# Sums of squared keys in four column groups, and two heads in turn in the products that complete T

## The chip, the cores and the metric

The kernel runs on one core of a Trainium2 chip. The core has a matrix engine (TensorE, PE in the profile; its weight loads are PEld), a vector engine (VectorE, DVE), a scalar engine (ScalarE, ACT), GpSimd (POOL), and SyncE (SP), which issues most transfers. The metric is the device time of one execution in microseconds, lower is better; where several runs are given, their median counts.

## What is computed

The reference is a trunk of two residual layers over 512 tokens of width 2048: one of gated differential attention, then one of RWKV-7 time mixing. Only the second layer is touched. It has 32 heads of 64 channels. Cut to what matters here:

```python
kk = heads(k * k_k)
kk = kk / jnp.maximum(jnp.sqrt(jnp.sum(kk * kk, axis=-1, keepdims=True)), 1e-12)
...
def step(S, inp):                       # per head, token after token
    sa = jnp.einsum('bhvk,bhk->bhv', S, a_t)          # a_t = -kk, b_t = kk * a
    S = S * w_t[:, :, None, :] + sa[..., None] * b_t[:, :, None, :] + v_t[..., None] * k_t[:, :, None, :]
    y = jnp.einsum('bhvk,bhk->bhv', S, r_t)
```

## The kernel before

The second layer goes through sixteen *pairs* of heads (`for j in range(D // P)` in `layer1`); a pair fills the 128 partitions, its first head on 0 to 63 and its second on 64 to 127. The 512 tokens are cut into `NC_` = 8 chunks of `C` = 64. For each pair there are:

- four projections of 128 channels (`unit_chan`, products in `mm3`, line 122), each 48 matmuls of 512 columns: fp32 numbers are split into a high and a low part of type fp32r (`split_w`, L105 on ACT and L106 on DVE for weights), and three products are added;
- `stage1`, whose steps `decays`, `exponentials`, `queries`, `scales` and `keys` are put in a list `g.later` and issued one by one behind steps of the scan of the pair before; `keys` squares k (L1264) and splits the square (`split_act`, L1101 on ACT and L1102 on DVE);
- `gram`: it sums the squared keys over the channels of each head with a matrix of ones (`sum_channels`, L1210 and L1211), copies the sums to the tile `ssl` (L1291 on ACT), writes them to a DRAM buffer `ltd` with two transfers on SP (L1293), and then forms the products of keys and queries within each chunk (L1304, tiles `gp`), which ACT copies to `G` (L1311) and SP writes to `ltd` (L1316);
- `t_solve`: POOL loads `ltd` into `LT` (L1350), and DVE divides by the sums (L1352, L1353) and inverts two triangular blocks of 32 per chunk in 31 steps (L1361, L1363). The result goes to DRAM (L1365);
- `t_combine`, one pair later: it loads the blocks into `TT`, transposes them (L1388), and forms the block below the diagonal with two runs of 32 x 32 products: L1394 into `px`, ACT copies to `X` (L1397), L1404 into `px`, ACT copies to `TT` (L1407). ACT also copies `AR` into `G` (L1400), over values that L1394 reads;
- `scan_pair`: for each chunk three products in a row, L1475 (`sm`), L1486 (reads `rhs`, which ACT copies in L1478), L1493, with L1488 on ACT and L1497 on DVE (L1500 for the first chunk) between them; then the outputs (L1515, L1519) and their normalisation.

`t_combine` and `scan_pair` are a `Chain`: they are issued in steps, each after a given number of matmuls of the projections, so that they stand among them on TensorE. From the fifth pair on the steps are placed so that L1394 of one pair, then the sums and L1304 of the next pair, then L1404 stand next to each other, ahead of the first L1475 of the scan.

The order of instructions on each engine is fixed when the kernel is built: a planner takes the instructions by priority (`high_priority`: weights 2000, the chain 3000, the solve and `ssl` 4000, all else by program order) when its own estimate of the times says that they can start; `issue_after` puts an instruction behind another one on its engine. Tiles with one tag share a buffer: `k2`, `ssl` and the `th` of `gate` have the tag `thg` with one buffer, and the split of k2 and that of r times k share `xH` and `xL`.

Of the kernel before, what the change touches and what calls it, by code (L numbers as in the profile page):

```python
# [13 lines left out]
F32 = mybir.dt.float32  # L14
# [3 lines left out]
AF = mybir.ActivationFunctionType  # L18
# [5 lines left out]
P = 128  # L24
D = 2048
T = 512
KT = D // P
NT = T // P
# [1068 lines left out]
def split_act(g, src, pool, tag):  # L1097
    nc = g.nc
    hh = pool.tile(list(src.shape), F32R, name="sH" + tag, tag=tag + "H", bufs=1)
    hl = pool.tile(list(src.shape), F32R, name="sL" + tag, tag=tag + "L", bufs=1)  # L1100
    nc.scalar.copy(hh[:], src)  # L1101
    nc.vector.tensor_sub(hl[:], src, hh[:].bitcast(F32))  # L1102
    return hh, hl
# [33 lines left out]
C = 64  # L1137
NC_ = T // C
HALF = 32
# [67 lines left out]
def sum_channels(g, out, ones, x):  # L1207

    h, l = x
    g.nc.tensor.matmul(out, ones, h[:], start=True, stop=False)  # L1210
    g.nc.tensor.matmul(out, ones, l[:], start=False, stop=True)  # L1211


def stage1(g, j, k, up):


    nc, w = g.nc, g.work
    p = Pair()
    col = lambda n: g.prm[n][:, j : j + 1]
    ch = lambda ap: ap.rearrange("p (c t) -> p c t", c=NC_)  # L1220
    th = []
    for i, nm in enumerate(("hw0", "ha0")):
        (uH, uL), (xH, xL) = up, g.dwda[i]
        ps = g.ps.tile([P, 512], F32, name="pt", tag="pb", bufs=2)
        mm3(nc, ps[:], uH[:, i, :], uL[:, i, :], xH[:], xL[:], True, True)
        o = w.tile([P, T], F32, name=f"th{i}", tag=f"th{i}", bufs=1)
        nc.scalar.activation(o[:], ps[:], AF.Tanh, bias=col(nm), scale=0.5)
        th.append(o)
    lw, tha = th
    nc.scalar.activation(lw[:], lw[:], AF.Identity, bias=g.hdec[:], scale=-0.5 * DECAY)  # L1230
    l = w.tile([P, NC_, C], F32, name="l", tag="l", bufs=1)
    m = g.small.tile([P, NC_], F32, name="m", tag="m", bufs=3)
    p.E = w.tile([P, NC_, C + 1], F32, name="E", tag="E", bufs=1)
    p.gam = g.small.tile([P, NC_], F32, name="gam", tag="gam", bufs=3)
    p.AR = w.tile([P, NC_, 2, C], F32, name="AR", tag="AR", bufs=3)
    p.BK = w.tile([P, NC_, 2, C], F32, name="BK", tag="BK", bufs=1)
    p.f = w.tile([P, T], F32, name="f", tag="f", bufs=1)

    def decays():
        nc.vector.tensor_tensor_scan(l[:].rearrange("p c t -> p (c t)"), g.rmask[:].rearrange("p c t -> p (c t)"),  # L1240
                                     lw[:], 0.0, ALU.mult, ALU.add)
        nc.vector.tensor_scalar(m[:], l[:, :, C - 1], 0.5, None, ALU.mult)
        nc.vector.tensor_sub(l[:], l[:], m[:, :, None].to_broadcast([P, NC_, C]))

    def exponentials():
        nc.scalar.activation(p.E[:, :, 0], m[:], AF.Exp, scale=-1.0)
        nc.scalar.activation(p.E[:, :, 1:], l[:], AF.Exp)
        nc.scalar.activation(l[:], l[:], AF.Exp, scale=-1.0)
        nc.scalar.activation(p.f[:], tha[:], AF.Identity, bias=col("omka"), scale=col("hka"))

    def queries():
        nc.vector.tensor_mul(p.f[:], p.f[:], k[:])
        nc.vector.scalar_tensor_tensor(p.AR[:, :, 0, :], ch(k[:]), col("nkk"), p.E[:, :, 0:C], ALU.mult, ALU.mult)
        nc.vector.tensor_mul(l[:], ch(k[:]), l[:])

    def scales():
        for i in range(2):
            nc.scalar.activation(p.BK[:, :, i, :], ch(tha[:]), AF.Identity, bias=col(f"bk_b{i}"),
                                 scale=col(f"bk_s{i}"))

    def keys():
        nc.vector.tensor_mul(p.BK[:], p.BK[:], l[:, :, None, :].to_broadcast([P, NC_, 2, C]))
        k2 = w.tile([P, T], F32, name="k2", tag="thg", bufs=1)
        nc.scalar.activation(k2[:], k[:], AF.Square, scale=col("kk"))  # L1264
        p.k2 = split_act(g, k2[:], w, "x")
        nc.vector.tensor_add(p.gam[:, 0 : NC_ - 1], m[:, 0 : NC_ - 1], m[:, 1:NC_])
        nc.scalar.activation(p.gam[:, 0 : NC_ - 1], p.gam[:, 0 : NC_ - 1], AF.Exp)

    g.later += [(0, decays), (1, exponentials), (0, queries), (1, scales), (1, keys)]
    return p  # L1270

# [12 lines left out]
def gram(g, j, p, before):  # L1284

    nc, w, BK = g.nc, g.work, p.BK
    ps = g.ps.tile([P, 512], F32, name="pt", tag="pa", bufs=1)
    sum_channels(g, ps[:2, :], g.ones[:, 0 : P : C], p.k2)
    ss = w.tile([2, T], F32, name="ssl", tag="thg", bufs=1)
    with g.tc.high_priority(offset=SOLVE):  # L1290
        nc.scalar.copy(ss[:], ps[:2, :])  # L1291
        for half in range(2):
            nc.sync.dma_start(  # L1293
                out=g.ltd[j % 2, half, :, :, HALF, :],
                in_=ss[:].rearrange("h (c b t) -> h c b t", c=NC_, b=2)[:, :, half, :])
    p.G = w.tile([P, NC_, 2, 2, C], F32, name="G1", tag="G1", bufs=2)
    p.BKT = w.tile([P, NC_, P], F32, name="BKT", tag="BKT", bufs=2)
    halves = []
    for c0, tag in ((0, "pb"), (4, "pc")):
        gp = [g.ps.tile([P, 512], F32, name="gp", tag=tag, bufs=2) for _ in range(2)]  # L1300
        halves.append((c0, gp))
        for i in range(4):
            for h, r_ in ((0, slice(0, C)), (1, slice(C, P))):
                m = nc.tensor.matmul(gp[h][:, i * P : (i + 1) * P], BK[r_, c0 + i, :, :], p.AR[r_, c0 + i, :, :],  # L1304
                                     start=True, stop=True)
    if before:
        with g.tc.issue_after(m.ins):
            before.step(g)
    for c0, gp in halves:
        for h in range(2):  # L1310
            nc.scalar.copy(p.G[:, c0 : c0 + 4, :, h, :], gp[h][:].rearrange("p (u x t) -> p u x t", u=4, x=2))  # L1311
    with g.tc.high_priority(offset=SOLVE if j == D // P - 1 else 0):
        for half in range(2):
            for h in range(2):
                q0 = h * C + half * HALF
                nc.sync.dma_start(  # L1316
                    out=g.ltd[j % 2, half, h, :, 0:HALF].rearrange("c s t -> s c t"),
                    in_=p.G[q0 : q0 + HALF, :, 0, h, half * HALF : (half + 1) * HALF])
# [53 lines left out]
def t_combine(g, j, p, lead):  # L1372

    nc, w, TT = g.nc, g.work, g.TT[j % 2]
    for h in range(2):
        for half in range(2):
            o, l0 = half * HALF, half * 16 + h * NC_
            nc.sync.dma_start(
                out=TT[h * C + o : h * C + o + HALF, :, h, o : o + HALF],
                in_=g.td[j % 2].rearrange("q (g l) t -> (q g) l t", g=NG)[:, l0 : l0 + NC_, :])  # L1380
    T1 = w.tile([P, NC_, HALF], F32, name="T1", tag="T1", bufs=1)
    X = w.tile([P, NC_, HALF], F32, name="X", tag="X", bufs=1)
    px = g.ps.tile([P, 512], F32, name="px", tag="pd", bufs=1)
    yield lead
    for h in range(2):
        r_ = slice(h * C, h * C + C)
        with g.tc.issue_after(g.centred) if g.centred else ExitStack():
            nc.vector.transpose(T1[r_], TT[r_, :, h, 0:HALF])  # L1388
    yield GAP_T
    N = NC_ * HALF  # L1390
    blocks = [(h, h * C, slice(h * C, h * C + HALF), slice(h * C + HALF, h * C + C)) for h in range(2)]
    for h, b0, lo, hi in blocks:
        for c in range(NC_):
            nc.tensor.matmul(px[hi, c * HALF : (c + 1) * HALF], p.G[lo, c, 0, h, HALF:C], T1[lo, c, :],  # L1394
                             start=True, stop=True, tile_position=(b0, b0 + HALF))
    for _, _, _, hi in blocks:
        nc.scalar.copy(X[hi], px[hi, :N].rearrange("p (c s) -> p c s", c=NC_))  # L1397
    for h, b0, _, _ in blocks:
        r_ = slice(b0, b0 + C)
        nc.scalar.copy(p.G[r_, :, 0, h, :], p.AR[r_, :, 0, :])  # L1400
    yield GAP_X
    for h, b0, lo, hi in blocks:
        for c in range(NC_):
            nc.tensor.matmul(px[lo, N + c * HALF : N + (c + 1) * HALF], X[hi, c, :], TT[hi, c, h, HALF:C],  # L1404
                             start=True, stop=True, tile_position=(b0 + HALF, b0))
    for h, b0, lo, _ in blocks:
        nc.scalar.copy(TT[lo, :, h, HALF:C], px[lo, N:].rearrange("p (c s) -> p c s", c=NC_))  # L1407
    yield GAP_T
# [363 lines left out]
```

## Time and profile before

| | |
|---|---|
| runs | 2114.43, 2110.9, 2113.84 us; median 2113.84 |
| profiled execution | 2111.84 us, of which the span from the first to the last instruction is 2110.1 |
| granted TensorE clock | 0.997 of full |
| busy, share of the span | PE 98%, PEld 80%, DVE 76%, ACT 55%, POOL 18% |
| the second layer's pairs | from 955 to 1960 us; a pair takes about 61.5 us from the fifth pair on |

The profile gives each instruction its line, engine, start and duration. In the timeline a row reads: start in us from the start of the span, duration in us, engine, line, operation, tiles written and read, partitions x elements, and the number of instructions that the row merges; in brackets stands the idle time of the engine before it and what ended it. A matmul's duration is its whole way through the array, and the next one starts before it ends, so what a matmul costs is read from one start to the next. A product in fp32 shows as two rows, two halves of the work; one in fp32r as one. "PEld ... LDWEIGHTS" is the load of a matmul's stationary operand.

### The profile page before, as it was taken

The page shows a single profiled execution, that of the slowest core. Times are in us where ns is not written, and L with a number is a line of the kernel's source. Part 1 is how long each engine was busy: PE and PEld are TensorE (multiplying, and loading weights), DVE is VectorE, ACT ScalarE, POOL GpSimd, SP SyncE. Part 2 cuts the span into 40 slices and gives each one's busy share as a digit, 9 for nine tenths or more (in the row PEclk, how much of TensorE's full clock was granted, in tenths as well). Part 3 has the DMA queues.
Part 4 walks back from the last instruction along what each step waited for, and adds up shares of the span by engine and source line. Part 5 has one row for each costly group of instructions (what it writes and reads, how often), then busy time and mean ns, then how long its engine had stood idle before and what let it go on. Part 6 is the DMA issues. An engine that isn't in the chain of part 4 may idle for free.

```text
span 2110.1 us, 34038 instructions
## 1 busy us (share of the span) xinstructions
PE 2076.8 (98%) x11852; PEld 1690.5 (80%) x11852; DVE 1602.6 (76%) x4129; ACT 1153.6 (55%) x2278; POOL 370.4 (18%) x727
## 2 busy tenths in 40 slices
PE   9999999999999999999999999999999999999999
PEld 7888888888887788878777778888877787877887
DVE  6988888889887876576777778877777887767645
ACT  5765656566565544355465555565555556555322
POOL 1021111201112000101122221222222122221001
PEclk9999999999999999999999999999999999999999
DMA  8487877878778946623232332323333232345655
GB/s 268 153 173 190 181 170 187 166 188 177 173 183 176 307 149 179 150 88 96 90 87 89 90 90 84 94 83 92 99 95 86 85 94 86 97 138 180 190 159 121
DMA packets 159484, 294.60 MB, mean 140 GB/s; under 512 B 64352, under 2 KB 81760, under 8 KB 159312
## 3 DMA queue, kind: packets, MB, share of 16 engines
q1 hardware_dynamic: 110848, 184.91, 28.1%
q0 software_dynamic: 23808, 83.54, 21.5%
q10 hardware_dynamic: 24656, 23.97, 3.5%
q8 instruction: 93, 1.52, 0.3%
q14 instruction: 79, 0.65, 0.1%
HBM read 268.71 MB, written 23.66 MB: 139 GB/s over the span
## 4 chain that ended last, share of the span: by engine, by line
PE 74%; DVE 17%; issue 3%; ACT 3%; DMA 2%; ACTq 0%; DVEq 0%; SPq 0%
PE pp L122 33%; PE pp L568 22%; PE pt L122 4%; DVE wl L106 4%; DVE tmpl L1361 3%; DVE Tm L1363 2%; DVE VS L1497 2%; PE gp L1304 1%; ACT wh L105 1%; PE sc L122 1%; PE o L122 1%; PE sm L1475 1%; PE lora L122 1%; PE z L122 1%; PE sm L1486 1%
## 5 line engine op out<-in xcount | busy, mean ns | idle before, releaser
L106 DVE TENSOR_TENSOR wl<-wraw,wh 128x1024 fp32r<-128x1024 f32 (+2 forms) x291 | 357.7, 1229 | 211.0 <-ACT wh L105 202.2
L105 ACT CAST wh<-wraw 128x1024 fp32r<-128x1024 f32 (+2 forms) x291 | 303.6, 1043 | 266.1 <-PE pp L122 135.2
L122 PE MATMUL pp<-hL,wh 128*128 128x512 f32 x1024 | 414.7, 405 | 0.0
L122 PE MATMUL pp<-hH,wh 128*128 128x512 f32 x1024 | 413.8, 404 | 0.0
L122 PE MATMUL pp<-hH,wl 128*128 128x512 f32 x1024 | 413.6, 404 | 0.0
L122 PEld LDWEIGHTS pp<-hH,wh 128*128 128x128 f32 x1024 | 193.6, 189 | 34.3
L122 PEld LDWEIGHTS pp<-hL,wh 128*128 128x128 f32 x1024 | 193.5, 189 | 33.3
L122 PEld LDWEIGHTS pp<-hH,wl 128*128 128x128 f32 x1024 | 193.6, 189 | 32.4
L568 PE MATMUL pp<-wh,hH 128*128 128x512 f32 x448 | 176.8, 395 | 0.0
L568 PE MATMUL pp<-wh,hL 128*128 128x512 f32 x448 | 175.8, 392 | 0.0
L122 PE MATMUL pp<-wh,hH 128*128 128x512 f32 x372 | 145.6, 392 | 1.8 <-ACT hH L1092 1.8
L122 PE MATMUL pp<-wh,hL 128*128 128x512 f32 x372 | 146.4, 394 | 0.2
L122 PE MATMUL pp<-wl,hH 128*128 128x512 f32 x372 | 145.9, 392 | 0.5 <-DVE wl L106 0.5
L1481 POOL COPY SA<-VS 64x64 f32<-64x64 f32 x224 | 69.9, 312 | 425.0 <-DVE VS L1497 386.0
L1361 DVE SCALAR_TENSOR_TENSOR tmpl<-LT,Tm 128x60 f32<-128x60 f32 (+24 forms) x496 | 133.6, 269 | 11.4
L568 PE MATMUL pp<-wl,hH 128*128 128x512 f32 x448 | 140.4, 392 | 0.0
L1363 DVE TENSOR_TENSOR Tm<-Tm,tmpl 128x60 f32<-128x60 f32 (+24 forms) x496 | 104.4, 211 | 11.3
L1478 ACT COPY rhs<-sm 64x64 f32<-64x64 f32 x256 | 52.8, 206 | 89.3 <-PE sm L1475 85.9
L568 PEld LDWEIGHTS pp<-wl,hH 128*128 128x128 f32 x448 | 84.4, 188 | 17.3
L568 PEld LDWEIGHTS pp<-wh,hH 128*128 128x128 f32 x448 | 84.2, 188 | 17.3 <-issue 0.3
L568 PEld LDWEIGHTS pp<-wh,hL 128*128 128x128 f32 x448 | 84.2, 188 | 16.3
L1488 ACT COPY VS<-sm 64x64 f32<-64x64 f32 x256 | 52.7, 206 | 71.9 <-PE sm L1486 67.3
(397 smaller groups left out, 4417.6 us busy)
## 6 DMA issues: line engine op xcount, KB each, us to landing
wraw<-in_rw_w_in_dram SPq DMA_DIRECT2D x128, 512.0 KB
wraw<-in_da_w_in_dram SPq DMA_DIRECT2D x75, 512.0 KB
wraw<-in_da_w_in_dram POOLq DMA_DIRECT2D x28, 512.0 KB, 6.6
wraw<-in_da_w_out_dram SPq DMA_DIRECT2D x26, 512.0 KB
wraw<-in_rw_w_out_dram SPq DMA_DIRECT2D x26, 512.0 KB
Ta<-in_da_w_in_dram POOLq DMA_DIRECT2D x21, 512.0 KB, 5.5
Tb<-in_da_w_in_dram POOLq DMA_DIRECT2D x21, 512.0 KB, 5.5
Tc<-in_da_w_in_dram POOLq DMA_DIRECT2D x21, 512.0 KB, 5.5
```

The source lines that it names most:

```text
L105: a = nc.scalar.copy(hi[:, ks], raw[:, ks])
L106: d = nc.vector.tensor_sub(lo[:, ks], raw[:, ks], hi[:, ks].bitcast(F32))
L122: m = nc.tensor.matmul(out, a, b, start=s, stop=e, skip_group_check=skip)
L568: m = nc.tensor.matmul(out[t][:], x, wt[lo][:, k, :], start=first, stop=end and lo == 1 and k == KG - 1, skip_group_check=True)
L1304: m = nc.tensor.matmul(gp[h][:, i * P : (i + 1) * P], BK[r_, c0 + i, :, :], p.AR[r_, c0 + i, :, :], start=True, stop=True)
L1361: nc.vector.scalar_tensor_tensor(tt, LT[:, i : i + 1, i + 1 :].to_broadcast([P, s, n]), n2[:, i : i + 1], Tm[:, 0:s, i : i + 1].to_broadca ...
L1363: nc.vector.tensor_add(Tm[:, 0:s, i + 1 :], Tm[:, 0:s, i + 1 :], tt)
L1475: nc.tensor.matmul(sm[:, 0:P], both(p.G[:, c, 0]), both(VS[:, c]), start=True, stop=True)
L1478: nc.scalar.copy(rhs[r_, :], sm[r_, h * C : h * C + C])
L1481: nc.gpsimd.tensor_copy(p.SA[r_, c - 1, :], VS[r_, c, h, :])
L1488: g.copied = nc.scalar.copy(VS[r_, c, h, :], sm[r_, P : P + C])
L1497: g.state = nc.vector.scalar_tensor_tensor(VS[r_, c + 1, h, :], s_, p.gam[r_, c : c + 1], Sg[r_, :], ALU.mult, ALU.add)
```

## The change

Two things are changed in the second layer.

The squared keys are no longer split into two fp32r parts. They stay fp32, in a tile of their own (`k2`), and are summed by four fp32 products, one for each 128 tokens, instead of two fp32r products over 512 tokens. Each product has 32 columns of the ones matrix as its stationary operand (16 for each head) and goes to its own group of 32 columns of the array, so that the sums of tokens 128 t to 128 t + 127 land on partitions 32 t to 32 t + 31. The copy `ssl` is then 128 partitions x 128 elements, also in a tile of its own, and the two transfers to `ltd` take one head each, from four partitions, instead of one half of each chunk.

In `t_combine` the loops of the two runs of products are exchanged: chunk after chunk, and in each the first head, then the second, instead of all chunks of the first head before those of the second. The products themselves and their places are the same.

```diff
     def keys():
         nc.vector.tensor_mul(p.BK[:], p.BK[:], l[:, :, None, :].to_broadcast([P, NC_, 2, C]))
-        k2 = w.tile([P, T], F32, name="k2", tag="thg", bufs=1)
-        nc.scalar.activation(k2[:], k[:], AF.Square, scale=col("kk"))
-        p.k2 = split_act(g, k2[:], w, "x")
+        p.k2 = w.tile([P, T], F32, name="k2", tag="k2", bufs=1)
+        nc.scalar.activation(p.k2[:], k[:], AF.Square, scale=col("kk"))
...
     ps = g.ps.tile([P, 512], F32, name="pt", tag="pa", bufs=1)
-    sum_channels(g, ps[:2, :], g.ones[:, 0 : P : C], p.k2)
-    ss = w.tile([2, T], F32, name="ssl", tag="thg", bufs=1)
+    for t in range(NT):
+        nc.tensor.matmul(ps[t * 32 : t * 32 + 32, :P], g.ones[:, C - 16 : C + 16].bitcast(F32),
+                         p.k2[:, t * P : (t + 1) * P], start=True, stop=True, tile_position=(0, t * 32))
+    ss = w.tile([P, P], F32, name="ssl", tag="ssl", bufs=1)
     with g.tc.high_priority(offset=SOLVE):
-        nc.scalar.copy(ss[:], ps[:2, :])
-        for half in range(2):
+        nc.scalar.copy(ss[:], ps[:, :P])
+        for h in range(2):
             nc.sync.dma_start(
-                out=g.ltd[j % 2, half, :, :, HALF, :],
-                in_=ss[:].rearrange("h (c b t) -> h c b t", c=NC_, b=2)[:, :, half, :])
+                out=g.ltd[j % 2, :, h, :, HALF, :].rearrange("b (q c) t -> q c b t", q=NT),
+                in_=ss[16 * h : P : 32, :].rearrange("q (c b t) -> q c b t", c=2, b=2))
...
-    for h, b0, lo, hi in blocks:
-        for c in range(NC_):
+    for c in range(NC_):
+        for h, b0, lo, hi in blocks:
             nc.tensor.matmul(px[hi, c * HALF : (c + 1) * HALF], p.G[lo, c, 0, h, HALF:C], T1[lo, c, :],
                              start=True, stop=True, tile_position=(b0, b0 + HALF))
...
-    for h, b0, lo, hi in blocks:
-        for c in range(NC_):
+    for c in range(NC_):
+        for h, b0, lo, hi in blocks:
             nc.tensor.matmul(px[lo, N + c * HALF : N + (c + 1) * HALF], X[hi, c, :], TT[hi, c, h, HALF:C],
                              start=True, stop=True, tile_position=(b0 + HALF, b0))
```

## The prediction

> **What bounds the kernel now.** I read the page first, then busy time by stretches, then the waits, then the timeline of one period.
>
> ```profile
> PE 2076.8 (98%) x11852; PEld 1690.5 (80%) x11852; DVE 1602.6 (76%) x4129; ACT 1153.6 (55%) x2278; POOL 370.4 (18%) x727
> 1434.00:1495.50 61.50, 60.82 (x422) 49.39 (x420) 46.48 (x133) 35.00 (x78) 15.24 (x35) 1.00 0.30 90
> PE sm L1475 <- DVE VS L1497: 7.6, 22, 0.6
> ```
>
> The second row is one pair of heads of layer two: 61.5 us, PE (first count) busy for 60.8, DVE (third) 46.5, ACT (fourth) 35.0. The third row is the only wait of PE that the waits view lists from 1188 to 1860 us, 7.6 us in eleven periods. So TensorE looks like the bound, and what the change takes from it should come off the time. Before adding that up I looked at the stretch in which the changed lines run:
>
> ```profile
> 1495.43 0.39 PE L122 MATMUL pp<-hH,wl 128*128 128x512 f32 x1
> 1495.75 1.09 PE L1394 MATMUL px<-T,G 32*32 32x32 f32 x32
> 1496.48 0.62 ACT L1400 COPY G<-AR 64x512 f32<-64x512 f32 x1 [3.15 <-PE px L1394]
> 1496.78 0.40 PE L1210 MATMUL pt<-sHx,ones 128*2 128x512 f32 x1
> 1497.01 0.40 PE L1211 MATMUL pt<-sLx,ones 128*2 128x512 f32 x1
> 1497.12 0.36 ACT L1397 COPY X<-px 32x256 f32<-32x256 f32 x1
> 1497.34 2.06 PE L1304 MATMUL gp<-AR,BK 64*128 64x128 f32 x32
> 1497.51 0.57 ACT L1291 COPY ssl<-pt 2x512 f32<-2x512 f32 x1
> 1498.11 0.36 ACT L1397 COPY X<-px 32x256 f32<-32x256 f32 x1
> 1498.49 0.61 ACT L1400 COPY G<-AR 64x512 f32<-64x512 f32 x1
> 1499.13 0.62 ACT L1101 CAST sHx<-mixr 128x512 fp32r<-128x512 f32 x1
> 1499.32 1.09 PE L1404 MATMUL px<-TT,X 32*32 32x32 f32 x32
> 1499.77 2.05 ACT L1311 COPY G<-gp 128x512 f32<-128x512 f32 x4
> 1500.34 0.50 PE L122 MATMUL pp<-hH,wh 128*128 128x512 f32 x1
> 1501.68 0.74 ACT L1407 COPY TT<-px 32x256 f32<-32x256 f32 x2
> 1502.45 1.05 ACT L105 CAST wh<-wraw 128x1024 fp32r<-128x1024 f32 x1
> 1503.53 0.42 ACT L1478 COPY rhs<-sm 64x64 f32<-64x64 f32 x2
> 1503.68 0.40 PE L122 MATMUL pp<-hL,wh 128*128 128x512 f32 x1
> 1504.00 0.43 PE L1486 MATMUL sm<-rhs,TT 128*128 128x64 f32 x2
>   PEld sm L1486: 3.7, 10
> ```
>
> ACT waits once, for the products of L1394, starts at 1496.48, and then has one copy behind the other until rhs is written at 1503.95: 7.47 us, nothing idle. L1486 reads rhs and starts at 1504.00. The last row, from the view of L1478 from 1250 to 1860 us, says that this happens in each of the ten pairs there. A matmul of L122 comes 0.23 us after the one before (1497.01 behind 1496.78 is the same 512 columns), so L1486 was due at 1503.91: TensorE is held by 0.09 us only. In this stretch the two engines arrive together, and a saving on TensorE alone turns into a wait for rhs.
>
> **The products that complete T.** Each run is 16 products in two halves, so 32 rows. L1394 takes from 1495.75 to 1496.78, 1.03 us; L1404 takes 1.02. Head after head they stand in one tile of the array for 16 rows, then in another.
>
> ```profile
> 1188.11 0.69 PE L1394 MATMUL px<-T,G 32*32 32x32 f32 x16
> 1188.72 0.40 PE L1210 MATMUL pt<-sHx,ones 128*2 128x512 f32 x1
> ...
> 1505.72 0.38 PE L1493 MATMUL sm<-VS,BKT 128*128 128x128 f32 x2
> 1505.94 0.60 PE L1336 MATMUL pt<-ident,BK 128*128 128x128 f32 x4
> ```
>
> One head alone occupies 0.61 us (1188.11 to 1188.72). Do two tiles run at once? A half of 128 columns over the whole array costs 0.11 us (two from 1505.72 to 1505.94). The gram products L1304, same columns but alternating between the two halves of the rows, take 1.98 us for 32, 0.062 each: two at a time. With heads in turn I expect the same here: 0.62 us a run instead of 1.03 and 1.02, so 0.41 + 0.40 off. If they don't overlap, nothing comes off.
>
> **The squared keys.** L1210 and L1211 hold TensorE from 1496.78 to 1497.34, 0.56 us. The new form has eight halves of 128 columns in four column groups. No row shows four column groups; the bounds are one at a time, 8 x 0.11 + 0.1 for the switch to L1304 (1497.34 less 1497.01 less 0.23), 0.98 us, and all four at once, 2 x 0.11 + 0.1, 0.32 us. L1304, which overlaps as far as it can, is nearest, so I take 0.32: some 0.2 off; the other end is 0.42 on. Together TensorE is 1.0 us ahead when it comes to L1486, at 1502.9.
>
> **ACT in the same stretch.** ssl becomes 128 columns on 128 partitions; now it is 0.57 us for 512 columns on two.
>
> ```profile
> L367 ACT CAST at<-pt 128x128 fp32r<-128x128 f32 x8 | 2.1, 267 | 8.6 <-PE pt L364 8.6
> ```
>
> That copy of 128 x 128 out of PSUM takes 0.27 (bounds: L1478 with 64 columns 0.21, L1407 with 256 columns 0.37): 0.31 off, rounded. ACT's start does not move: the first head's last product still starts after 16 steps. Then rhs is ready at 1503.64 and L1486 starts near 1503.69 instead of 1504.00. Of TensorE's 1.0 us, 0.31 reaches the end; the other 0.7 becomes a wait in front of L1486. The split of k on ACT and DVE goes too, but elsewhere:
>
> ```profile
> L1101 ACT CAST sHx<-k x16: 604/616/621, 961.2 to 1851.5; 128x512 fp32r<-128x512 f32 x16
> L1102 DVE TENSOR_TENSOR sLx<-k,sHx x16: 677/678/693, 963.4 to 1852.5; 128x512 fp32r<-128x512 f32 x16
> 1482.27 0.72 ACT L1264 ACTIVATE k<-mixk,prm_kk 128x512 f32<-128x512 f32 x1 [0.82 <-DVE mixv L1441]
> 1513.32 0.60 DVE L1497 SCALAR_TENSOR_TENSOR VS<-sm,gam,Sg 64x64 f32<-64x64 f32 x2 [0.34 <-PE sm L1493]
> 1513.95 0.18 DVE L1352 TENSOR_SCALAR LT<-LT 128x32 f32<-128x32 f32 x1
> ```
>
> 0.62 of ACT and 0.68 of DVE, 16 times each. In the steady pairs they follow L1264, when the last state of the scan is formed, and no wait of TensorE comes between them and the next L1394, so I cost their going at nothing; without that cover they would give 0.6 a pair. L1264 no longer waits for L1441 (they shared a tile) and can move into ACT's gap before it: nothing, or up to 0.72 if it lands ahead of an rhs copy. The freed split buffer also lets the cast of r (L1101, 0.62) start before L1400 instead of after. It would push L1400 back by some 0.36 and leave the chain behind, 0.26 better: kept for the range. The two DMAs a pair from ssl carry as many 128-byte rows from four partitions as from one run of 512 before; those of G follow them, so they set nothing. Behind L1486 all shifts together: the solve on DVE (L1352) stands behind L1497, which itself waited for TensorE (0.34), and the waits of L1475 come from that solve.
>
> **The sum.** Twelve pairs have this form (the ten of the row above, one before, one behind): 12 x 0.31 = 3.7 us. In the first pairs the T of the pair before is completed among matmuls of L122, with no gram beside it:
>
> ```profile
> 1025.42 1.09 PE L1394 MATMUL px<-T,G 32*32 32x32 f32 x32 [1.15 <-DVE y L1418]
> 1026.79 0.63 PE L122 MATMUL pp<-hL,wh 128*128 128x512 f32 x1
> ...
> 1029.78 0.58 PE L122 MATMUL pp<-hH,wl 128*128 128x512 f32 x1
> 1164.31 0.46 PE L1475 MATMUL sm<-VS,G 128*128 128x128 f32 x2 [0.81 <-DVE VS L1497]
> 1164.85 0.39 PE L122 MATMUL pp<-hL,wh 128*128 128x512 f32 x1
> ```
>
> Three such pairs give 3 x 0.81 = 2.4 us on TensorE, the four first sums some 0.1 each (0.24 less one more switch), and 0.68 less on DVE inside the first solve shortens the 1.15 us wait: 3.5 at most, and nothing if waits on DVE like the 0.81 above swallow it. I take 3.0, an estimate near the upper end, because the 1.15 itself gets shorter and the 0.81 is one of few. At the tail one run of L1404 stands among L122: 0.4. Sum: 3.7 + 3.0 + 0.4 = 7.1 us.
>
> The profiled execution took 2111.84 us, its span 2110.1, so 1.7 lie around it; the sum makes it 2104.7. It ran 2.0 below the median of the runs, 2113.84. Against that median the forecast is 2113.84 - 7.1 = 2106.7. From the bounds, 3.7 + 0 + 0 gives 2110.1, and with the cast of r ahead (12 x 0.26 = 3.1 more) it is 2103.6; the forecast's own range is 2103 to 2110. I call 0.2%, 4.2 us, what a measurement of this kernel can tell from no change.
>
> **Rivals.** *TensorE's whole gain arrives.* L105, 1.05 us on ACT, stands ahead of rhs. The order on ACT comes from the planner, and if it sees rhs in time and puts it first, rhs is ready at 1502.6 and L1486 goes at 1502.9: 1.0 a pair, 12.0 + 3.4 = 15.4, so 2098.4. For it: L1475, whose product rhs copies, would come 1.0 us earlier. Against it: the planner put L105 first here, and nothing says that it prices the products by their overlap.
>
> *The heads do not overlap.* Both heads write the same tile px in PSUM, while the heads of L1304 write different ones. If writes into one bank exclude each other, a run stays at 1.03 us, the first head now ends with the second, and L1400 starts 0.40 later: ACT gains 0.31 and loses 0.40, 12 x 0.09 = 1.1 us lost, some 0.6 won by sums in the first pairs, 2114.3: no change. [...] The trace speaks against it: one head is busy for 0.69 us, and 16 more starts at the step of 1.03 / 32 = 0.032 would make it 1.20; L1394 with both heads shows 1.09. Where the rows of one head meet the other's, they ran together, in one bank.
>
> *Slower: the clock falls.* In the rows above the eight matmuls from 1026.79 to 1029.78, behind a wait of 1.15 us, come 0.43 apart instead of 0.23, 0.2 us more each; behind 0.81 the next keeps its 0.39. Counted as those rows do, from the end of the matmul before, the forecast's wait is 1503.69 less (1503.68 - 1.0 + 0.40), 0.6. From somewhere between 0.81 and 1.15 it would cost 8 x 0.2 = 1.6 us a pair, 19 in all; with the 3.4 of the first pairs and the tail, 2113.84 + 19.2 - 3.4 = 2129.6 (rhs itself then comes no earlier). That needs ACT's chain to stay as long as it is, by ssl not getting cheaper on 128 partitions. [...]
>
> *The change doesn't do what it says.* If the planner sends all of one head before the other, as at 1188.11, where 16 rows of one head are followed by L1210, L1394 keeps its time. That differs from the second rival only in that L1400 does not start later: 12 x 0.31 and little else, within the forecast's range.
>
> **How the numbers follow.** Forecast 0.58, since the chain on ACT is measured pair by pair. Whole gain 0.18, no overlap 0.14, clock 0.10. The range is 2097.5 to 2114.5 us: it takes in the first two rivals with a spread of a microsecond, and leaves out the clock and tails of the rest. Faster by over 0.2%, below 2109.6: 0.55 of the forecast and 0.18 of the whole gain, 0.73. Within 0.2%: 0.03 and 0.13, 0.16. Slower by over 0.2%, above 2118.1: 0.11.
>
> **What would show it.** In the changed profile L1394 and L1404 should be busy 0.70 us in 32 rows and be followed by the next line after 0.62. The sums should show eight rows within 0.32 us; if 0.9, the column groups ran in turn, which the wait at L1486 would hide. ssl should take 0.27. The first L1486 of a pair should start right behind rhs, some 1.0 us after the matmul before it (0.32 now), and the order on ACT should be L105 and then rhs. The time from one pair's L1394 to the next should shrink by 0.3 us. It is wrong if rhs stands before L105 (then by 1.0), if L1400 starts later than 0.73 us behind the first L1394, or if L122 behind L1486 takes 0.63.

## The result

| | before | after |
|---|---|---|
| median of the runs | 2114.14 us (2110.9 to 2116.03, 4 runs) | 2100.53 us (2099.12 to 2102.03, 4 runs) |
| profiled execution, its span | 2111.84, 2110.1 us | 2100.14, 2098.4 us |

The ratio is 0.9939, with a 95% interval from 0.9927 to 0.9951: 13.6 us faster, 11.7 between the two profiled executions. The forecast was 7.1 us, 2106.7. The time lies in the stated range (2097.5 to 2114.5), but below the forecast's own 2103 to 2110, and only 2.1 us from the 2098.4 of the rival by which TensorE's whole gain arrives. So the time alone does not tell which mechanism held; the traces have to.

### The profile after

From line 1266 up to the sums, line numbers are one lower than before (`mixr` is written in L1279, not L1280), and behind the sums one higher: L1288 is the line of the sums, L1292 `ssl`, L1305 the gram products, L1395 and L1405 the products that complete T, L1398, L1401 and L1408 the copies around them, L1476, L1479, L1487 the scan.

First the page's line of busy times, then a pair by stretches (columns as before: PE, PEld, DVE, ACT, POOL), then the waits of PE from 1182 to 1850 us.

```profile
PE 2061.8 (98%) x11948; PEld 1678.3 (80%) x11948; DVE 1590.7 (76%) x4113; ACT 1139.1 (54%) x2262; POOL 372.0 (18%) x727
1494.90:1555.77 60.87, 59.85 (x428) 48.66 (x426) 45.60 (x129) 34.16 (x78) 15.29 (x36) 1.00 0.33 92
PE sm L1476 <- DVE VS L1498: 7.4, 22, 0.5
PE sm L1487 <- ACT rhs L1479: 4.2, 11, 0.6
```

The last row is the new one. Before, PE had one wait here; now it waits in eleven pairs for `rhs` as well. In the pair of the second row PE is idle for 1.0 us of 60.87, where it was idle for 0.7 of 61.50: TensorE's work got shorter by 1.0 us, the pair by 0.6.

The stretch of the prediction, one period of the changed kernel (timeline):

```profile
1548.82 0.69 PE L1395 MATMUL px<-T,G 32*32 32x32 f32 x32
1549.31 0.62 ACT L1101 CAST sHx<-mixr 128x512 fp32r<-128x512 f32 x1 [2.91 <-DVE mixr L1279]
1549.45 0.42 PE L1288 MATMUL pt<-k,ones 128*32 128x128 f32 x8
1549.80 2.06 PE L1305 MATMUL gp<-AR,BK 64*128 64x128 f32 x32
1549.94 0.27 ACT L1292 COPY ssl<-pt 128x128 f32<-128x128 f32 x1
1550.23 0.74 ACT L1398 COPY X<-px 32x256 f32<-32x256 f32 x2
1550.99 1.26 ACT L1401 COPY G<-AR 64x512 f32<-64x512 f32 x2
1551.79 0.69 PE L1405 MATMUL px<-TT,X 32*32 32x32 f32 x32
1552.28 2.06 ACT L1312 COPY G<-gp 128x512 f32<-128x512 f32 x4
1552.41 0.50 PE L122 MATMUL pp<-hH,wh 128*128 128x512 f32 x1
...
1554.19 0.74 ACT L1408 COPY TT<-px 32x256 f32<-32x256 f32 x2
1554.95 1.05 ACT L105 CAST wh<-wraw 128x1024 fp32r<-128x1024 f32 x1
...
1555.76 0.40 PE L122 MATMUL pp<-hL,wh 128*128 128x512 f32 x1
1556.03 0.42 ACT L1479 COPY rhs<-sm 64x64 f32<-64x64 f32 x2
1556.50 0.43 PE L1487 MATMUL sm<-rhs,TT 128*128 128x64 f32 x2 [0.34 <-ACT rhs L1479]
```

L1395 is busy for 0.69 us in 32 rows and followed after 0.63 (1549.45); L1405 likewise (1551.79 to 1552.41). The sums hold TensorE for 0.35 us (1549.45 to 1549.80). ACT has again one copy behind the other until `rhs` ends at 1556.45, and L1487 starts 0.05 us later, 0.74 behind the matmul before it. What the forecast did not have as its main case is the second row: the cast of r (L1101) stands at the head of ACT's chain and begins 0.49 us behind L1395, in time in which ACT was idle. Before, the first G copy began 0.73 behind L1394, with that cast behind it.

The executions of one kernel differ by more than the terms that are argued about here: on one chip the kernel before ran from 2108.95 us (mean granted clock 0.999) to 2119.95 us (0.994). So below I compare stretches of the traces, cut at starts of the same instructions: *first pairs*, from the first L1304 of the second layer to the fifth pair's L1394; *period*, a tenth of the time from there to the L1394 ten pairs on; *chain*, from L1394 to the first L1486 in these pairs; *wait*, from the start of the matmul before that L1486 to its start (0.23 is none), both as medians of the ten; *tail*, from the L1394 that closes the ten pairs to the end. In the ten pairs every version with the old sums has TensorE's instructions in the order of the kernel before, and every version with the new sums in that of the changed kernel, but for the two loops. Two values of a stretch are from two profiles of one kernel. The runs are of two series on two chips, each with 17 runs of the kernel before (2113.73 and 2112.67); the ratios below are each to its own.

| kernel | runs, median us | first pairs | chain | wait | period | tail |
|---|---|---|---|---|---|---|
| before / again | 2113.73, 2112.67 | 280.60 / 280.55 | 8.25 / 8.26 | 0.33 / 0.33 | 61.41 / 61.42 | 245.9 / 247.0 |
| heads in turn alone / again | 2106.37 | 278.15 / 278.20 | 8.24 / 8.24 | 1.12 / 1.11 | 61.40 / 61.37 | 242.7 / 247.1 |
| sums alone | 2106.94 | 277.19 | 8.09 | 0.35 | 61.23 | 245.4 |
| after / again | 2098.51 | 274.42 / 274.53 | 7.69 / 7.69 | 0.75 / 0.75 | 60.86 / 60.88 | 245.4 / 244.3 |
| after, cast of r behind | 2103.6 | 274.61 | 7.80 | 0.87 | 60.95 | 252.3 |
| after, ssl three times | 2106.65 | 275.48 | 8.15 | 1.21 | 61.34 | 245.0 |
| after, weights behind rhs / again | 2101.3 | 277.19 / 277.34 | 7.18 | 0.24 | 60.27 / 60.28 | 250.2 / 249.7 |
| after, G copies on POOL | 2094.94 | 276.93 | 7.18 | 0.24 | 60.28 | 243.1 |
| before, T later | 2112.9 | 278.04 | 8.26 | 0.33 | 61.41 | 251.6 |

The columns from first pairs to period repeat within 0.2 us; the tail does not. From before to after the first pairs give 6.0 to 6.2 us, the ten pairs 10 x 0.55 = 5.5. The rest of the difference lies in the tail and ahead of the second layer, and differs from execution to execution.

### The profile page after: what moved, and what is told of

Its sections match the earlier page's. It is cut to its first block, busy times and chain, and to the rows that moved or that the text cites. A ratio compares the mean times of both kernels' runs of the same rounds, so it can differ in the third digit from the quotient of the medians.

```text
span 2098.4 us, 34166 instructions
## 1 busy us (share of the span) xinstructions
PE 2061.8 (98%) x11948; PEld 1678.3 (80%) x11948; DVE 1590.7 (76%) x4113; ACT 1139.1 (54%) x2262; POOL 372.0 (18%) x727
## 3 DMA queue, kind: packets, MB, share of 16 engines
q8 instruction: 94, 1.54, 0.3%
## 4 chain that ended last, share of the span: by engine, by line
PE 71%; DVE 17%; ACT 5%; issue 4%; DMA 2%; ACTq 0%; DVEq 0%; SPq 0%; POOLq 0%
PE pp L122 32%; PE pp L568 22%; PE pt L122 4%; DVE wl L106 3%; DVE tmpl L1362 3%; DVE Tm L1364 2%; ACT wh L105 2%; DVE VS L1498 1%; PE gp L1305 1%; PE sc L122 1%; PE o L122 1%; PE sm L1476 1%; DMA ys<-yTl 1%; PE lora L122 1%; PE z L122 1%
## 5 line engine op out<-in xcount | busy, mean ns | idle before, releaser
L106 DVE TENSOR_TENSOR wl<-wraw,wh 128x1024 fp32r<-128x1024 f32 (+2 forms) x291 | 355.6, 1222 | 236.7 <-ACT wh L105 224.8
L105 ACT CAST wh<-wraw 128x1024 fp32r<-128x1024 f32 (+2 forms) x291 | 303.6, 1043 | 272.4 <-PE pp L122 131.9
L122 PE MATMUL pp<-hL,wh 128*128 128x512 f32 x1024 | 414.1, 404 | 0.0
L122 PE MATMUL pp<-hH,wh 128*128 128x512 f32 x1024 | 413.4, 404 | 0.0
L122 PE MATMUL pp<-hH,wl 128*128 128x512 f32 x1024 | 413.1, 403 | 0.0
L122 PEld LDWEIGHTS pp<-hH,wh 128*128 128x128 f32 x1024 | 193.1, 189 | 34.4 <-issue 0.2
L122 PEld LDWEIGHTS pp<-hL,wh 128*128 128x128 f32 x1024 | 193.1, 189 | 33.1
L122 PEld LDWEIGHTS pp<-hH,wl 128*128 128x128 f32 x1024 | 193.2, 189 | 32.4
L122 PE MATMUL pp<-wh,hH 128*128 128x512 f32 x372 | 146.5, 395 | 1.9 <-ACT hH L1092 1.9
L122 PE MATMUL pp<-wl,hH 128*128 128x512 f32 x372 | 146.7, 394 | 0.7 <-DVE wl L106 0.5
L122 PE MATMUL pp<-wh,hL 128*128 128x512 f32 x372 | 147.0, 395 | 0.2 <-DVE hL L1093 0.2
L1479 ACT COPY rhs<-sm 64x64 f32<-64x64 f32 x256 | 52.8, 206 | 101.5 <-PE sm L1476 98.3
```

Of the source, the lines that this page charges most:

```text
L105: a = nc.scalar.copy(hi[:, ks], raw[:, ks])
L106: d = nc.vector.tensor_sub(lo[:, ks], raw[:, ks], hi[:, ks].bitcast(F32))
L122: m = nc.tensor.matmul(out, a, b, start=s, stop=e, skip_group_check=skip)
L1479: nc.scalar.copy(rhs[r_, :], sm[r_, h * C : h * C + C])
```

## The experiments

The question is why a pair gives 0.55 us where TensorE was spared 1.0 and the forecast had 0.31, and why the first pairs give twice what was forecast. The theory on record is that ACT's chain decides when the first L1486 starts, whatever TensorE saves. Its rivals: that TensorE's saving counts as such, and that a longer wait lets the clock fall.

### Heads in turn alone

The kernel before, with only the two loops of `t_combine` exchanged:

```diff
-    for h, b0, lo, hi in blocks:
-        for c in range(NC_):
+    for c in range(NC_):
+        for h, b0, lo, hi in blocks:
```

> The kernel before with the loops of L1394 and L1404 exchanged and nothing else. Theory ACT (in each steady pair the chain of copies on ACT, from L1394 to rhs, decides when the first L1486 starts): ssl is still 0.57 us and all copies still stand ahead of rhs, so a pair still takes 61.4 us, the step from the last L122 to the first L1486 grows from 0.33 to about 1.1 us, and only the three first pairs and the tail gain, 3 x 0.81 + 0.4 = 2.8 us: 2111.3, ratio 0.9987. Theory TensorE (what TensorE is spared comes off): 12 x 0.81 + 2.8 = 12.5 us, 2101.6, ratio 0.9941.

Measured: 2106.37 us, ratio 0.997 [0.9958, 0.9982]. In the timeline of one period and, last, in the waits of PE from 1250 to 1850 us:

```profile
1494.92 0.69 PE L1394 MATMUL px<-T,G 32*32 32x32 f32 x32
1495.64 0.62 ACT L1400 COPY G<-AR 64x512 f32<-64x512 f32 x1 [3.15 <-PE px L1394]
1498.09 0.69 PE L1404 MATMUL px<-TT,X 32*32 32x32 f32 x32
1503.16 0.43 PE L1486 MATMUL sm<-rhs,TT 128*128 128x64 f32 x2 [0.72 <-ACT rhs L1478]
PE sm L1486 <- ACT rhs L1478: 7.2, 10, 0.7
```

TensorE saves its 0.8 us a pair, and all of it comes back as the wait of the last row: chain 8.24 and period 61.40, where they were 8.25 and 61.41. (ACT's order is another one here, with `ssl` directly behind the first G copy and the cast of r between the copies of `gp`; its sum is the same.) That refutes "TensorE's whole gain arrives" for this half of the change. The first pairs are 2.4 us shorter, most of it by matmuls that no longer run at half the clock (below). The whole comes out faster than expected. Part of that belongs to the execution: the tail was 242.7 us in the first profile and 247.1 in the second (below). Why all five runs came out between 2106 and 2108 us is open.

### Sums alone

The changed kernel with the two loops of `t_combine` put back, head after head (the diff above, reversed).

> The changed kernel with the old loop order in L1394 and L1404, so only the sums in fp32 with four column groups, and no split of k. The cast of r stands behind L1400 here, as before. Theory ACT: rhs comes 0.31 us earlier by ssl, TensorE is spared 0.24, so about 0.3 a pair, 12 x 0.3 = 3.6; in the first pairs the wait for T gets shorter by the split's 0.68 us on DVE and the clock no longer falls behind it (8 x 0.2 = 1.6), together 2.3: 2108.2, ratio 0.9972. Theory TensorE: 12 x 0.24 + 0.4 = 3.3 us, with nothing in the first pairs: 2110.8, ratio 0.9984. By either, the two halves of the change done alone add up to less than the change if the ACT order matters.

Measured: 2106.94 us, ratio 0.9972 [0.996, 0.9984]; period 61.23, first pairs 277.2. ACT's rows of one period:

```profile
1494.11 0.62 ACT L1401 COPY G<-AR 64x512 f32<-64x512 f32 x1 [3.15 <-PE px L1395]
1494.90 0.27 ACT L1292 COPY ssl<-pt 128x128 f32<-128x128 f32 x1 [0.17 <-PE pt L1288]
1495.19 0.74 ACT L1398 COPY X<-px 32x256 f32<-32x256 f32 x2
1495.95 0.62 ACT L1401 COPY G<-AR 64x512 f32<-64x512 f32 x1
1496.60 0.62 ACT L1101 CAST sHx<-mixr 128x512 fp32r<-128x512 f32 x1
```

`ssl` takes 0.27 us here too, but it stands behind the first G copy and waits 0.17 us for the sums, which come only when both heads' products are through; and the cast of r is behind the G copies, as before, although the buffer is free in this kernel too. A period gains 0.18. With 0.18 for the sums and none for the heads, the two parts alone make 0.2 us; together they make 0.55. They work on one chain: heads in turn bring the sums 0.4 us forward, so that `ssl` waits for nothing.

### The cast of r behind the G copies

The changed kernel, with the split of r put behind the second G copy on ACT:

```diff
-        nc.scalar.copy(p.G[r_, :, 0, h, :], p.AR[r_, :, 0, :])
+        g.kept = nc.scalar.copy(p.G[r_, :, 0, h, :], p.AR[r_, :, 0, :])
...
-                p.rfs = split_act(g, p.rf[:], w, "x")
+                with tc.issue_after(g.kept.ins) if g.kept else ExitStack():
+                    p.rfs = split_act(g, p.rf[:], w, "x")
```

> The changed kernel with the cast of r (L1101, sHx from mixr) kept behind the copies L1400, where it stood before, by an order on ACT alone. Theory ACT: the 0.62 us are back in the chain and L1400 may start 0.36 earlier, so rhs is 0.26 later and a pair takes 61.1 instead of 60.83 us: 12 x 0.26 = 3.1 us more than the change, 2103.6, ratio 0.9954. Theory TensorE: ACT's order is of no account, 2100.5, ratio 0.9939.

Measured: 2103.6 us, ratio 0.995 [0.9934, 0.9966]; period 60.95, chain 7.80.

```profile
1490.01 0.62 ACT L1401 COPY G<-AR 64x512 f32<-64x512 f32 x1 [3.15 <-PE px L1395]
1490.54 0.25 ACT L1292 COPY ssl<-pt 128x128 f32<-128x128 f32 x1
...
1492.22 0.62 ACT L1101 CAST sHx<-mixr 128x512 fp32r<-128x512 f32 x1
...
1497.09 0.43 PE L1487 MATMUL sm<-rhs,TT 128*128 128x64 f32 x2 [0.47 <-ACT rhs L1479]
```

The period is 0.09 us longer than with the cast ahead, the chain 0.11, not the 0.26 that was expected. The rows say why, step by step. In the changed kernel ACT's chain begins 0.49 us behind L1395 where it began at 0.73, 0.24 saved by the cast, and the step from `ssl` to the next copy is 0.29 where it was 0.60 (1550.23 less 1549.94; before, 1498.11 less 1497.51), 0.31 saved; all other steps are the same within 0.01, and the sum is 0.55. With the cast behind, the chain begins at 0.72 again, the step behind `ssl` is 0.27 (1490.81 less 1490.54), 0.33 saved, and a second thing has changed: `ssl` now stands directly behind the first G copy and starts 0.53 after it, where L1397 started 0.64 after it (1497.12 less 1496.48), 0.11 saved; in all 0.44, and the period says 0.46. So the edit took away the 0.24 of the cast and brought 0.13 of its own by the new order. The experiment confirms that the cast's place counts; it does not measure it cleanly. The times of the whole scatter (2098.16 to 2108.98); the profiled one had a tail of 252.3. That their median is the expected 2103.6 is chance, since the period lost a third of what was expected.

### ssl three times

The changed kernel, with the copy made three times, to lengthen the chain by about what the change took from it:

```diff
-        nc.scalar.copy(ss[:], ps[:, :P])
+        for _ in range(3):
+            nc.scalar.copy(ss[:], ps[:, :P])
```

> The changed kernel with the copy ssl (128 x 128, 0.27 us) done three times. Theory ACT: 0.54 us more ahead of rhs, the step to the first L1486 grows from 0.75 to 1.28 us, a pair takes 61.37 instead of 60.83: 12 x 0.54 = 6.5 us more than the change, 2107.0, ratio 0.9970. Theory TensorE: ACT is busy 55% of the time and has room, 2100.5, ratio 0.9939. If the wait, then about 0.9 us from the end of the matmul before, makes the clock fall, 1.6 us a pair come on top, near 2126.

Measured: 2106.65 us, ratio 0.9968 [0.9956, 0.998]; period 61.34, wait 1.21. The waits of PE from 1250 to 1850 us:

```profile
PE sm L1488 <- ACT rhs L1480: 8.6, 10, 1.1
PE sm L1477 <- DVE VS L1499: 6.8, 20, 0.5
```

(The edit moves the lines by one: L1488, L1480 and L1477 are L1487, L1479 and L1476.) Two more copies of 0.27 us lengthen the chain by 0.46 and the period by 0.48 (61.34 less 60.86), not by the 0.54 expected, because the G copy starts 0.16 behind the third `ssl`. TensorE and DVE run what they run in the changed kernel, in the same order, in these ten pairs; ACT has the added copies and nothing else. So ACT's chain sets the period in these pairs: shown, by an edit that touches nothing else there. The wait of 1.21 us from start to start is 0.81 counted as the prediction's rival counts it, from the end of the matmul before (longest 1.12). That reaches into the span from 0.81 to 1.15 where the rival was to begin, and let no clock fall in these ten pairs: in the period read the matmuls of L122 behind it start 0.22 to 0.24 us apart.

### The chain taken out of the way, twice

*The split of the weights behind rhs.* Each split of a weight (L105) that is issued after the scan's first chunk is put behind that chunk's `rhs` copy on ACT:

```diff
+            if g.rhs and not turn:
+                after.enter_context(g.tc.issue_after(g.rhs))
...
-            nc.scalar.copy(rhs[r_, :], sm[r_, h * C : h * C + C])
+            m = nc.scalar.copy(rhs[r_, :], sm[r_, h * C : h * C + C])
+        if c == 0:
+            g.rhs = m.ins
```

> The changed kernel with the weight cast L105 kept behind the first rhs copy of each scan, by an order on ACT alone; no work is added or removed. Theory ACT: rhs comes 1.05 us earlier, TensorE no longer waits at the first L1486 (step 0.23 instead of 0.75 us), a pair takes 60.3 instead of 60.83: 12 x 0.51 = 6.1 us less than the change, 2094.4, ratio 0.9907. Rival: the weight cast that is now later is needed just as soon, and TensorE waits for wh or wl instead: no gain, 2100.5, ratio 0.9939.

*The G copies on POOL:*

```diff
-        nc.scalar.copy(p.G[r_, :, 0, h, :], p.AR[r_, :, 0, :])
+        nc.gpsimd.tensor_copy(p.G[r_, :, 0, h, :], p.AR[r_, :, 0, :])
```

> The changed kernel with the two copies L1400 (AR into G, 0.62 us each on ACT) on GpSimd. Theory ACT: the chain ahead of rhs is 1.23 us shorter, more than the 0.51 that TensorE waits, so a pair takes 60.3 us as with rhs first: 2094.4, ratio 0.9907. Rival: GpSimd takes over a microsecond for each, L1475, which reads G, waits for them, and the load of LT queued behind them on GpSimd makes the solve later: 2100.5 or more, ratio 0.9939 or above.

Both bring the period to 60.27 and 60.28 us, with no wait left at the first L1487 (0.24). The second, in one period:

```profile
1488.67 1.31 POOL L1401 COPY G<-AR 64x512 f32<-64x512 f32 x2 [8.21 <-PE px L1395]
1489.03 0.27 ACT L1292 COPY ssl<-pt 128x128 f32<-128x128 f32 x1
...
1494.10 0.42 ACT L1479 COPY rhs<-sm 64x64 f32<-64x64 f32 x2
1495.09 0.33 PE L1487 MATMUL sm<-rhs,TT 128*128 128x64 f32 x2
```

`rhs` is there 0.57 us before L1487 (1495.09 less 1494.52), so the bound has gone back to TensorE. From 61.41 that is 1.13 us a pair: the 1.0 that the change takes from TensorE, and the 0.1 that TensorE waited here before. The 0.6 that the change left behind was this wait. The two copies take 1.31 us on POOL together, not over a microsecond each as the rival had it. The G copies on POOL measure 2094.94 us (2092.82 to 2096.88), ratio 0.9914 [0.9895, 0.9932]; this version beats both kernels. It would win more if its first pairs were not 2.5 us longer than those of the change (276.93 to 274.42), 0.8 of it by one new wait of TensorE for a copy of `VS` on ACT; the rest I have not taken apart.

The weights behind `rhs` win as much per pair and yet come to 2101.3 us, ratio 0.9944 [0.9928, 0.9961], no better than the change. Its first pairs are 2.8 us longer than those of the change, its tail 5 us. Two rows of PE, one from each (the edit adds two lines here: L124 is L122, L107 and L108 are L105 and L106):

```profile
1084.23 0.50 PE L124 MATMUL pp<-hH,wl 128*128 128x512 f32 x1 [0.53 <-DVE wl L108]
1915.42 0.80 PE L124 MATMUL pp<-wh,hH 128*128 128x512 f32 x1 [2.93 <-ACT wh L107]
```

There a projection waits for the weights that now stand behind `rhs`. That is the expectation's rival: it holds outside the ten pairs, and the first theory holds inside them. In the first pairs two such waits (0.53 and 0.66 us) make 1.2 of the 2.8; the rest I have not taken apart. The second profile has the same 2.92 us wait at 1915.75, and a tail of 249.7 after 250.2.

### The first T placed later

The kernel before, with the first pair's L1394 eight matmuls later (`leads = {1: 72, ...}` for 64), to take away the wait of 1.15 us without touching products or sums.

> The kernel before with the first pair's lead at 72 matmuls instead of 64, so that L1394 of pair 0 stands behind eight more matmuls of L122 and does not wait for its T. Theory clock: the wait of 1.15 us makes the following eight matmuls 0.2 us slower each; both go, 1.3 + 1.6 = 2.9 us: 2111.2, ratio 0.9986, with no matmul of 0.63 us in that stretch. Rival: the slow matmuls come from something else and stay, or the wait comes back later in the same chain: between nothing and 1.3 us, 2114.1 to 2112.8.

Measured: 2112.9 us, ratio 0.9999 [0.9988, 1.0009]. The wait and the 0.43-us steps behind it are gone (0.32 from start to start, then steps of 0.22 to 0.24), and the first pairs are 2.5 us shorter, but the whole isn't: a tail of 251.6 took more than that in this profile. What the first wait costs can be seen in the stretch, not in the whole.

### The same kernels again

The changed kernel a second time, and, since the tail and the clock seemed to belong to the execution, three kernels for a second profile.

> The changed kernel again, on the same chip as these, as the mark for them. Every theory: ratio 0.9939 within its interval, a pair 60.83 us.

> The kernel before, unchanged, for a second profile. Its runs so far lie between 2108.8 and 2120.8 us, the lower the higher their mean granted clock (0.999 at 2109, 0.995 at 2120). Theory A, that the slow matmuls belong to an execution and not to a kernel: pairs of 61.41 us again, and the two places that differ from profile to profile, the first pair's 0.43-us matmuls (8 of them so far) and the time from the last T (pair 14) to the end (245.9 so far), differ again, by some 1.5 and up to 7 us, while the time less these stays within 1 us. Theory B, that they are fixed by the order of the kernel: 8 slow matmuls behind the first wait for T, and 245.9 at the tail, within 0.5.

> Heads in turn alone, unchanged, for a second profile: its first gave 61.40 us a pair, a wait of 1.64 us (start to start) for the first T, no 0.43-us matmul and a tail of 242.7. Theory A (by execution): the same pair period, but slow matmuls may now stand behind the first T or in the tail, and the tail may be anything from 242.5 to 252. Theory B (by kernel): none, 242.7 within 0.5.

> The split of the weights behind rhs, unchanged, for a second profile: its first gave 60.27 us a pair, but 13 slow matmuls and a tail of 250.2. Theory A (by execution): 60.27 again, with a tail and a count of slow matmuls that are others; its other runs at 2099.7 with a clock of 0.998 would have a tail near 248. Theory B (by kernel): 13 and 250.2 within 0.5 again.

The changed kernel: 2098.51 us, ratio 0.9938 [0.992, 0.9957]. The table shows the rest. First pairs, chain and period belong to the kernel. The tail is mixed. In the kernel before and in the one with heads in turn alone it is the execution's, since the last pair's T came back from DRAM at different times: DVE was idle for 1.27 us ahead of L1388, the transpose of that T, until its transfer landed in one profile of heads in turn alone, and for 2.09 in the other. Two profiles of the kernel before (timeline of PE):

```profile
1921.24 0.69 PE L1394 MATMUL px<-T,G 32*32 32x32 f32 x16 [0.85 <-DVE T L1388]
...
1922.38 0.69 PE L1394 MATMUL px<-T,G 32*32 32x32 f32 x16 [1.95 <-DVE T L1388]
```

With heads in turn alone the wait there was 1.03 and then 1.85 us, and behind the longer one the clock fell. Stretches of the two profiles; the first number behind the five busy times is the granted clock:

```profile
1918.50:1921.40 2.90, 2.90 (x40) 2.19 (x39) 2.84 (x5) 0.93 (x2) 0.00 (x0) 1.00 0.46 92
1918.50:1921.40 2.90, 2.90 (x35) 2.04 (x34) 2.87 (x6) 0.86 (x2) 0.00 (x0) 0.50 0.64 165
```

The same code at a clock of 0.50. Of the 4.4 us between the tails 242.7 and 247.1, 0.8 is the longer wait; the rest comes with the 10.24 us at half the clock that begin behind it. With the weights behind `rhs` the tail repeated within 0.5; there it is the kernel's. And the slow matmuls behind the first T, 8 of them in the first profile of the kernel before, came again in the second (7).

## Why the prediction came out as it did

**The heads overlap: right, to a few hundredths.** 0.62 us a run was forecast, 0.63 and 0.62 were measured. The rival by which writes into one place in PSUM keep the heads apart is refuted: both heads write the tile `px`, and their 32 rows were busy for 0.69 us, as long as the 16 rows of one head before. That this tile is one bank, as the prediction puts it, no trace shows.

**The sums: right.** 0.32 us was taken, between 0.32 and 0.98, because L1304 was the nearest row; 0.35 was measured.

**ssl: right.** 0.27 us forecast and measured.

**ACT's chain decides: right, and shown** for the ten pairs, by ssl three times (TensorE unchanged, the period longer by as much as the chain), by heads in turn alone (TensorE shorter, the period unchanged), and by the G copies on POOL (the wait gone, 1.13 us a pair).

**What it gives per pair: mis-sized, 0.31 instead of 0.55.** The prediction had both numbers: 0.31 with ACT's order as it was, and 0.26 more with the cast of r ahead of L1400, 0.57. It took the first for the sum and kept the second for the range. The second came: 0.31 from `ssl` and 0.24 from the cast, by the steps on ACT. The step that failed is the choice between them. ACT's idle time of 3.15 us before L1400 stood in the quoted rows, and by the prediction's own word it was the shared buffer that held the cast back; whether the planner would use the free buffer could not be read from the trace: with sums alone, where it is free too, the cast stayed last. So the two orders were two cases of like weight, and the prediction gave one of them no share in its sum. Twelve pairs at 0.24 are 2.9 us of the miss.

**The first pairs: mis-sized.** Forecast were 3.0 us for the three pairs with the early form and 0.31 for the one of the later form that lies in the same stretch; measured were 6.1. By parts: from the first L1304 to the first L1394 0.7 us (55.93 to 55.20), from there to the third gram 2.5 (48.89 to 46.40), from there to the fifth L1394 3.0 (175.78 to 172.82). The middle one can be taken apart. Heads in turn alone gives 2.3 there, sums alone 1.6, and one thing is in both: the matmuls behind the first T no longer run at half the clock. Rows of stretches, before and after:

```profile
1026.80:1030.10 3.30, 3.30 (x9) 2.62 (x8) 2.88 (x4) 2.21 (x5) 1.41 (x2) 0.50 0.25 69
1026.80:1030.10 3.30, 3.30 (x44) 2.54 (x43) 1.81 (x3) 2.69 (x6) 2.84 (x3) 1.00 0.63 188
```

The prediction saw these eight matmuls, used them as the price of a rival, 8 x 0.2 = 1.6 us, and did not ask whether the change would take them away. With 2 x 0.4 for the two runs of products between these points that makes 2.4 of the 2.5. This is the term that was missing. The wait itself went from 1.54 to 0.75 us, from start to start, but a shorter wait is not needed to spare the matmuls: with heads in turn alone it was 1.64 and 1.69, and they were spared too. What spares them is open (last section). Of the last stretch, 0.55 is the pair of the later form; heads in turn alone gives only 0.2 there, and sums alone 1.3, against 1.6 and some 0.2 forecast for what lies in it. Which waits take the one and give the other I have not taken apart. The 0.4 us forecast for the tail can't be read, since two profiles of one kernel differ there by up to 4.4.

**The clock as the slower rival: not met.** The wait at L1487 came out at 0.75 from start to start, which is 0.35 in the prediction's count, from the end of the matmul before; and nothing fell: the granted clock from 1246 to 1860 us was 1.00. The point from which that rival was said to decide, between 0.81 and 1.15 us in that count, isn't supported: the waits of 1.25 and 1.30 with heads in turn alone (the 1.64 and 1.69 just named) passed at full clock (1.00 around the first of them, second row of the last section; the first pairs of the two profiles agree, 278.15 and 278.20), and so did shorter ones ten times over, of 0.72 there and 0.81 (median) with ssl three times. Where the clock fell in the second layer, the wait ahead of it was never under 1.09 (1.47 from start to start; the kernel before, second profile), but one of 1.95 in the tail of that same profile passed, with the matmuls of L122 behind it 0.23 apart. The length of one wait does not decide it.

**TensorE's whole gain: not met, for the reason given.** `rhs` stayed behind L105. Where it is taken from there, the gain arrives in these pairs.

## What to carry to other kernels

Where two engines arrive at one instruction within 0.1 us of each other, cut the chain of the second before counting on the first: 0.8 us saved on TensorE were worth nothing a pair alone; 1.0 saved were worth 0.55 with one copy on ACT shortened and a cast moved into its idle time, and 1.13 with another 1.3 us of copies moved to an idle engine. When an edit frees a buffer, look for what stood behind it and for an idle stretch of its engine in front: a planner may fill that, and the order after the edit is a case with its own price, not a margin. And when executions of one kernel differ by more than the effect, cut the traces at the same instructions: the stretches here repeat within 0.2 us where the totals differ by 11.

## What the hardware showed unasked

- Four products in four column groups of 32 columns, each in two halves, went through in 0.35 us, the switch to the next line included; eight halves one after the other would have been 0.98 by the prediction's own bound, an estimate from 0.11 us for a half over the whole array and 0.1 for the switch.
- Falls of the granted clock to 0.50 lasted, by the trace's record of the clock, 3.41 us (before, from 1026.75), 6.83 (before, from 685.41, and weights behind rhs, first profile), 10.24 (heads in turn alone, second profile) and 13.65 (cast of r behind): one, two, three and four times 3.413. TensorE was not idle all the time ahead of the first of these: PE was busy for 2.25 of the 3.40 us ahead of the fall from 1026.75, in the first row here, of the kernel before.

```profile
1023.30:1026.70 3.40, 2.25 (x38) 1.71 (x37) 2.00 (x4) 1.30 (x2) 2.23 (x5) 1.00 0.73 234
1025.49:1028.90 3.41, 2.16 (x40) 1.52 (x38) 1.64 (x3) 1.66 (x2) 2.63 (x6) 1.00 0.70 221
```

- In the first profiles of the kernels before and after all falls begin and end whole lengths of 3.413 us apart, but for the end of the one that the record cuts off. In the kernel before they begin at 685.41, 1026.75 and 2108.77, the second 100 and the third 417 lengths behind the first; in the changed kernel at 21.42, 687.02 and 2096.72, 195 and 608 lengths behind the first.
- Why a wait of 1.54 us lets the clock fall and one of 1.64 doesn't is open. The second row above takes in that longer wait, from the first profile of heads in turn alone: PE was busy for less of it, 2.16 us of 3.41, and the clock stayed at 1.00. What differs is the work: 38 instructions of PE lie in the first row, 40 in the second. Whether the amount of work decides is not shown; no run varied it alone.
- On ACT the step behind a G copy of 0.62 us was not the same for each copy that followed: `ssl` started 0.53 us behind it (cast of r behind), L1397 0.64 (before). No run asked why.
